# Powers of the query and key norms by logarithm and exponential on ScalarE, and the causal mask put on the logarithms

## The chip, the cores and the metric

The kernel runs on one core of a Trainium2 chip. A core has TensorE (PE in the profile; PEld is its weight load), VectorE (DVE), ScalarE (ACT), GpSimd (POOL) and SyncE (SP), each with a queue of its own that is worked off in order, and 16 DMA engines. The metric is device time in microseconds, lower is better; shown are the median of the runs of the kernel before and one execution taken by the hardware profiler.

## The reference, cut to what matters

One layer of a decoder trunk on 512 tokens of width 2048, all in float32. The part that the change touches is the attention branch with its two norms (8 heads of 128 features, blocks of 128 queries):

```python
def rmsnorm(x, g):
    y = x * lax.rsqrt(jnp.mean(x * x, axis=-1, keepdims=True) + EPS)
    return y * g

q = rmsnorm(q.reshape(B, S, 8, 128), q_norm_g)
k = rmsnorm(k.reshape(B, S, 8, 128), k_norm_g)

# stick-breaking attention, for one block of queries
z = einsum('bhqd,bhkd->bhqk', qi, kf) * 128 ** -0.5
strict = key_pos[None, :] < q_pos[:, None]
log_beta = log_sigmoid(z)
log_1m = where(strict, log_sigmoid(-z), 0)
tail = cumsum(log_1m, axis=3, reverse=True) - log_1m
w = where(strict, exp(log_beta + tail), 0)
out = einsum('bhqk,bhkd->bhqd', w, vf)
```

Around it stand a combined projection `w_in` (9216 columns: u, v_sgu, q, k, v_att and two gates), a gated spatial branch, the merge through `w_up_a`, `w_up_b` and `w_o`, a feed-forward block with 5632 hidden units, and a gated embedding.

## The kernel before, in words

Everything is kept transposed: features on the 128 partitions, the 512 tokens along the free dimension. A matrix product works on pairs of 128 output rows. Each float32 operand is split into a high part, copied to the fp32r type by ScalarE, and a low part, the rest, formed by VectorE; a product is the sum of three matmuls (high by high, high by low, low by high). Most products run on blocks with seven multiplications in place of eight (`PRODUCTS`, `HALVES`), whose sums of activations and weights VectorE forms; one sum of two weight blocks is formed by a DMA that adds into its destination (`landed`, L351, issued from GpSimd's queue once the first part of the weights has landed). `high`, `sums` and `rest` are the other steps of a piece of weights: L347 on ScalarE is the high part, L363 the sums, L344 the low part on VectorE. `mix_doubled` (L751 on ScalarE, L754 on VectorE) takes the seven products out of PSUM.

The projection goes first, for 56 pairs of output rows. The order is four rounds, each a pair of q (two heads), of k, of v and then three or four pairs of gates; after the rounds come the pairs of the gated spatial branch. The attention of a round runs beside the matmuls of the pairs that follow. Its steps are generators (`q_prep`, `k_prep`, `v_prep`, `attention`), and each `yield n` puts the next step n ticks later; there are eight ticks to a pair. Instructions that a tick issues are kept behind the matmuls issued before it. Within these limits the engines' orders come from a planner that estimates the duration of each instruction and gives a free engine the earliest step in the text whose inputs it reckons to be there. So the order on an engine can differ from the order in the text.

- `q_prep`: `flip` (L1032) transposes one head's queries so that tokens lie on partitions; `squares` (L1039) lets ScalarE square and sum each of the four blocks of tokens; `token_rms` forms the mean plus epsilon on VectorE (L1047) and raises it to the power -0.5 on GpSimd (L1049); VectorE multiplies the result by 128 ** -0.5 (L1064); one tick later `times` (L1054) scales the queries on ScalarE; two ticks later they are transposed back and ScalarE multiplies them by the gain (L1071).
- `k_prep` does the same for the keys up to the power, which is kept in `rk` and used as the scale of the logits (L1109, L1110). The first norm's epsilon is carried as `eps_cols`, four columns made once from the mean of squares of x (L1302), since the rows of x are not scaled ahead of the projection.
- `attention` goes through blocks of 128 keys, the last first, with the keys on partitions and the queries that can see the block along the free dimension. `stage_a` (L1107 to L1112) makes z and log(1 + exp(-|z|)). `stage_m` makes the logarithm of the weight `w` (L1116) and the sum term `s` (L1118) on VectorE; GpSimd sets s to zero where a key is not ahead of its query (L1120), copies one row out (L1127) and clears it (L1128). `stage_b` (L1131) and `stage_c` (L1135) split s into high and low parts; `stage_d` sums it over keys with a triangular matrix on TensorE (L1141, L1142), carries a row to the next block (L1144), subtracts the sums from w (L1146) and takes the exponential (L1147); GpSimd sets the weight to zero where the mask says so (L1148). `finish` multiplies the four blocks of weights with the values (L1157) and copies the result out (L1159).

PSUM has two banks for all small products of attention and six for the projection. The table set that ScalarE loads at the start is `natural_log_exp_and_others` (L852).

Of the kernel before, what the change touches and what calls it, by code (L numbers as in the profile page):

```python
# [12 lines left out]
F32 = mybir.dt.float32  # L13
F32R = mybir.dt.float32r
AF = mybir.ActivationFunctionType
ALU = mybir.AluOpType
# [3 lines left out]
P = 128  # L20
T = 512
NT = T // P
# [5 lines left out]
GROUPS = 8  # L28
PLE = 256
EPS = 1e-6  # L30

OUT = "SSSSPPPP"
PASSES = "SSSSSSSS", "SSSSSSSS", "SSSSPP"
# [34 lines left out]
def hybrid_layer(  # L68
# [18 lines left out]
    nc = tc.nc  # L87

    consts = ctx.enter_context(tc.tile_pool(name="consts", bufs=1))
# [810 lines left out]
    def load_x():  # L900
# [18 lines left out]
                            fill=0.0, base=0, channel_multiplier=1)  # L919
# [3 lines left out]
    expo = consts.tile([P, 8], F32, name="expo")  # L923
# [67 lines left out]
    norm1 = Norm()  # L991
# [32 lines left out]
        return att[tag].f(start, start + n)  # L1024

    eps_cols = consts.tile([P, NT], F32, name="eps_cols")

    def flip(o):

# [10 lines left out]
                                 accum_out=ms[:, t : t + 1])  # L1040
        return ms

    def token_rms(ps, r):

        norm1.row()
        ms = squares(ps)
        nc.vector.scalar_tensor_tensor(out=ms, in0=ms, scalar=1.0 / P, in1=eps_cols,  # L1047
                                       op0=ALU.mult, op1=ALU.add)
        nc.gpsimd.tensor_tensor(out=r, in0=ms, in1=expo[:, :NT], op=ALU.pow)  # L1049

    def times(dst, ps, r):
        for t in range(NT):
# [3 lines left out]
    def q_prep(o, i):  # L1056


        for h in range(2):
            yield 2  # L1060
            ps = flip(o[:, h * T : (h + 1) * T])
            q, r = take(T), rms_tile()[:, :NT]
            token_rms(ps, r)
            nc.vector.tensor_scalar(out=r, in0=r, scalar1=float(P) ** -0.5, scalar2=None,  # L1064
                                    op0=ALU.mult)
            yield 1
            times(q.f(), ps, r)
            yield 2
            if not h:
                y_b[i] = take(1024)  # L1070
            nc.scalar.activation(y_b[i].f(h * T, (h + 1) * T), flip(q.f()), AF.Copy,  # L1071
                                 scale=gcol[:, g_q : g_q + 1])
            give(q)
# [12 lines left out]
    def attention(rnd, kT, rk, v):  # L1086
        state = {}
        yield 1
        qT = y_b[rnd].f()
        zh, zl = (att[t].own() for t in ("zh", "zl"))  # L1090

        def sums(j):
            return a_tile("zs", (NT - j) * P, j % 2 * T)

        def weights(h, j):
            return a_tile(f"w{j}", (NT - j) * P, (j == NT - 1) * h * P)

        def first(j):

            return (sums(j) if j == NT - 1 else a_tile("first", (NT - j) * P, (j == 1) * 2 * P))[0:1]  # L1100

        def stage_a(h, j):
            n = (NT - j) * P
            r = rk[:, 4 * h + j : 4 * h + j + 1]
            z = small_bank()[:, :n]
            c = h * T + j * P
            nc.tensor.matmul(z, kT[:, c : c + P], qT[:, c : (h + 1) * T], start=True, stop=True)  # L1107
            l, s = a_tile("l")[:, :n], sums(j)
            nc.scalar.activation(l, z, AF.Abs, scale=r)  # L1109
            nc.scalar.activation(s, z, AF.Copy, scale=r)  # L1110
            nc.scalar.activation(l, l, AF.Exp, scale=-1.0)
            nc.scalar.activation(l, l, AF.Ln, bias=1.0)  # L1112

        def stage_m(h, j):
            l, s, w = a_tile("l")[:, : (NT - j) * P], sums(j), weights(h, j)
            nc.vector.scalar_tensor_tensor(out=w, in0=s, scalar=0.0, in1=l,  # L1116
                                           op0=ALU.min, op1=ALU.subtract)
            nc.vector.scalar_tensor_tensor(out=s, in0=s, scalar=0.0, in1=l,  # L1118
                                           op0=ALU.max, op1=ALU.add)
            nc.gpsimd.affine_select(out=s[:, :P], in_=s[:, :P], pattern=[[1, P]],  # L1120
                                    compare_op=ALU.is_gt, fill=0.0, base=0,
                                    channel_multiplier=-1)


            if j < NT - 1:
                if j:
                    nc.gpsimd.tensor_copy(first(j), s[0:1])  # L1127
                nc.gpsimd.memset(s[0:1, :P], 0.0)  # L1128

        def stage_b(j):  # L1130
            nc.scalar.activation(zh[:, : (NT - j) * P], sums(j), AF.Copy)  # L1131

        def stage_c(j):
            n = (NT - j) * P
            in_turn(nc.vector.tensor_tensor(out=zl[:, :n], in0=sums(j), in1=att["zh"].f(0, n),  # L1135
                                            op=ALU.subtract))

        def stage_d(h, j):
            n, w = (NT - j) * P, weights(h, j)
            tp, t = small_bank()[:, :n], tris[j < NT - 1]  # L1140
            nc.tensor.matmul(tp, t, zh[:, :n], start=True, stop=False)  # L1141
            nc.tensor.matmul(tp, t, zl[:, :n], start=False, stop=True)  # L1142
            if j:
                nc.vector.tensor_tensor(out=sums(j - 1)[0:1, P:], in0=tp[0:1], in1=first(j),  # L1144
                                        op=ALU.add)
            nc.vector.tensor_tensor(out=w, in0=w, in1=tp, op=ALU.subtract)  # L1146
            nc.scalar.activation(w, w, AF.Exp)  # L1147
            nc.gpsimd.affine_select(out=w[:, :P], in_=w[:, :P], pattern=[[1, P]],  # L1148
                                    compare_op=ALU.is_gt, fill=0.0, base=0,
                                    channel_multiplier=-1)  # L1150
            state[h, "w", j] = w

        def finish(h):
            y = small_bank()
            for j in range(NT):
                c = h * T + j * P
                nc.tensor.matmul(y[:, j * P :], v[:, c : c + P], state.pop((h, "w", j)),  # L1157
                                 start=j == 0, stop=j == NT - 1)
            nc.scalar.activation(qT[:, h * T : (h + 1) * T], y, AF.Copy)  # L1159
            if h == 1:  # L1160
                nc.sync.dma_start(out=y_spill[rnd], in_=qT)
                give(y_b[rnd])
                y_done["b", rnd] = True

        blocks = [(h, j) for h in range(2) for j in range(NT - 1, -1, -1)]
        stage_a(*blocks[0])
        yield 1
        stage_m(*blocks[0])
        yield 1
        stage_a(*blocks[1])  # L1170
        for i, (h, j) in enumerate(blocks):
            ahead = blocks[i + 1 : i + 3]
            stage_b(j)
            yield 1
            if i == NT:
                finish(0)
            stage_c(j)
            if ahead:
                stage_m(*ahead[0])
            yield 1  # L1180
            stage_d(h, j)
            if ahead[1:]:
                stage_a(*ahead[1])
            yield 1
        yield 1
        finish(1)
        if rnd == 3:
            for tag in ("first", "k", "v", "zs", "zh", "zl"):
                give(att.pop(tag))

    def sgu_v(rnd, o):

        for h in range(2):
# [10 lines left out]
            ssq = squares(ps)  # L1204
            nc.vector.tensor_scalar(out=ssq, in0=ssq, scalar1=1.0 / P, scalar2=EPS,
                                    op0=ALU.mult, op1=ALU.add)
# [92 lines left out]
    for n, ((w, i), pr) in enumerate(zip(order, made())):  # L1299
        if n == 0:  # L1300
            row1 = norm1.row()
            nc.vector.tensor_scalar(out=eps_cols, in0=norm1.mean, scalar1=EPS, scalar2=None,  # L1302
                                    op0=ALU.mult)
        if n == 0:
            a_tiles()
        o = pr.out(block(w, i) if n < 3 else None)
        if w == "q":
            beside(q_prep(o, i))
        elif w == "k":
            kT, rk = o, rms_tile()  # L1310
            beside(k_prep(kT, rk))
            beside(attention(i, kT, rk, a_tile("v", 1024)), 6)
        elif w == "v":
            beside(v_prep(o, a_tile("v", 1024)))
        elif w == "s":
            scaled(o, row1)
            nc.scalar.activation(o, o, AF.Gelu_apprx_tanh)
            beside(sgu_v(i, o))
        elif w == "u":
            scaled(o, row1)  # L1320
            nc.scalar.activation(o, o, AF.Gelu_apprx_tanh)
            nc.vector.tensor_tensor(out=y_a[i].f(), in0=o, in1=y_a[i].f(), op=ALU.mult)
            y_done["a", i] = True
        else:
            d = tc.dram_tile([P, 1024], F32, name=nm("gsp"))
            nc.sync.dma_start(out=d, in_=o)
            gate_spill[w, i] = d
# [5 lines left out]
    ms = [form(k, lambda j=j: merged[j], lambda j=j: j in merged, raw=0, **how)  # L1333
          for j, k in enumerate(OUT) for how in [{} if k == "S" else {"how": "high"}]]
# [232 lines left out]
```

## Time and profile before

| | us |
|---|---|
| median of 3 runs | 2690.93 |
| lowest, highest | 2689.34, 2696.23 |
| profiled execution | 2691.74 |
| its span, first to last instruction | 2690.0 |

How to read the profile: "busy" is the sum of an engine's instruction times; a matmul's end is modelled. In a table of stretches, the columns are the length, the busy time of PE, PEld, DVE, ACT and POOL with counts, the clock that TensorE was granted as a share of full speed, the share of the DMA engines' time and GB/s. In a row of waits stand the engine that waited, tile and line, what released it, then total us, times and the longest. A row of the timeline has start, duration, engine, line, instruction, shapes, count, and in brackets the idle time ahead of it with its releaser. A row of a group has count, busy us and mean ns of one, then the idle time of the engine ahead of it. A row of one line's durations has the lowest, median and highest in ns. An engine's idle time costs nothing where it isn't the one that sets the end.

### The profile page before, as it was taken

To read this page: it belongs to the slowest core of one execution; us is meant where nothing else is said; L and a number is where in the kernel's file an instruction comes from. 1 tells how busy PE (TensorE), PEld (TensorE's weight loads), DVE (VectorE), ACT (ScalarE), POOL (GpSimd) and SP (SyncE) were. 2 spreads that over 40 slices of the span, in tenths; PEclk is the share of its full clock that TensorE was granted. 3 is DMA by queue.
4 is the path that set the end of the run, shared out by engine and by line. 5 is a ranking of instruction groups with operands and counts; after the bars stand their busy time and mean duration, and the time that the engine had idled before them with its cause. 6 is when DMAs were issued, how large, how long until landed. Compare 5 with 4: busy or idle time off the path is not lost.

```text
span 2690.0 us, 42553 instructions
## 1 busy us (share of the span) xinstructions
PE 2653.3 (99%) x15496; PEld 2325.7 (86%) x15496; DVE 2207.7 (82%) x3715; ACT 1388.7 (52%) x2161; POOL 458.2 (17%) x549
## 2 busy tenths in 40 slices
PE   8999999999999999999999999999999999999999
PEld 7889898889898889988888888888888888888898
DVE  8687878787887666688898888888899889889876
ACT  7656565655554334375444444444445444444543
POOL 0223323232220000001111111111110111100010
PEclk9999999999999999999999999999999999999999
DMA  7677777777776457667888888888888979978884
GB/s 226 154 185 175 182 173 184 172 183 198 174 187 196 140 164 211 178 210 198 230 212 213 204 202 200 201 206 199 207 197 244 259 213 279 259 254 259 257 248 126
DMA packets 288241, 548.62 MB, mean 204 GB/s; under 512 B 25888, under 2 KB 138272, under 8 KB 288032
## 3 DMA queue, kind: packets, MB, share of 16 engines
q1 hardware_dynamic: 229232, 441.03, 50.3%
q0 software_dynamic: 58800, 104.88, 25.2%
q8 instruction: 121, 1.98, 0.3%
q14 instruction: 88, 0.72, 0.1%
HBM read 498.63 MB, written 47.19 MB: 203 GB/s over the span
## 4 chain that ended last, share of the span: by engine, by line
PE 85%; DVE 7%; DMA 3%; ACT 2%; issue 2%; POOL 1%; SPq 0%; DVEq 0%; ACTq 0%; POOLq 0%
PE ps L695 47%; PE ps L285 10%; PE ps L286 10%; PE ps L284 10%; PE small L695 6%; DVE wlo L344 2%; DVE out L754 1%; DMA wholes<-x 1%; DVE parts L275 1%; PE small L1157 1%; DMA wholes<-hid 1%; DVE wholes L363 1%; ACT whi L347 1%; DVE wholes L513 1%; PE small L1032 1%
## 5 line engine op out<-in xcount | busy, mean ns | idle before, releaser
L695 PE MATMUL ps<-parts,whi 128*128 128x512 f32 x3960 | 1324.8, 397 | 0.3 <-DVE p L754 0.3
L347 ACT ACTIVATE whi<-wholes 128x512 fp32r<-128x512 f32 (+3 forms) x933 | 866.0, 942 | 787.0 <-DVE wholes L363 274.0
L344 DVE TENSOR_TENSOR wlo<-wholes,whi 128x512 fp32r<-128x512 f32 (+3 forms) x933 | 974.1, 1078 | 85.6 <-ACT whi L347 85.4
L695 PEld LDWEIGHTS ps<-parts,wlo 128*128 128x128 f32 x3960 | 743.7, 188 | 168.1 <-issue 1.0
L695 PE MATMUL ps<-parts,wlo 128*128 128x256 f32 x3960 | 784.3, 279 | 0.1
L285 PE MATMUL ps<-parts,whi 128*128 128x256 f32 (+1 forms) x2070 | 679.5, 329 | 4.8 <-DVE parts L275 4.7
L284 PE MATMUL ps<-parts,whi 128*128 128x256 f32 (+1 forms) x2048 | 668.1, 328 | 12.4 <-ACT parts L274 10.6
L286 PE MATMUL ps<-parts,wlo 128*128 128x256 f32 (+1 forms) x2070 | 677.6, 329 | 1.7 <-DVE wlo L344 1.7
L695 PEld LDWEIGHTS ps<-parts,whi 128*128 128x128 f32 x3960 | 637.8, 189 | 5.9 <-issue 1.0
L285 PEld LDWEIGHTS ps<-parts,whi 128*128 128x128 f32 x2070 | 393.6, 190 | 46.5 <-DVE parts L275 7.3
L284 PEld LDWEIGHTS ps<-parts,whi 128*128 128x128 f32 x2048 | 388.5, 190 | 48.9 <-ACT parts L274 12.7
L286 PEld LDWEIGHTS ps<-parts,wlo 128*128 128x128 f32 x2070 | 393.5, 190 | 36.2 <-DVE wlo L344 3.2
L363 DVE TENSOR_TENSOR wholes<-wholes 128x256 f32<-128x256 f32 (+1 forms) x806 | 338.9, 420 | 19.1 <-issue 1.7
L754 DVE TENSOR_TENSOR out<-out,ps 128x256 f32<-128x256 f32 x460 | 190.8, 417 | 150.9 <-ACT out L751 150.2
L351 POOL DMA_DIRECT2D wholes<-w_ffn_in x172 | 150.1, 872 | 689.1 <-DVE wholes L363 251.7
L351 POOL DMA_DIRECT2D wholes<-w_in x132 | 118.3, 898 | 484.4 <-DMA wholes<-w_in 133.7
L695 PE MATMUL small<-parts,whi 128*128 128x512 f32 x440 | 174.5, 397 | 0.0
L275 DVE TENSOR_TENSOR parts<-wholes,parts 128x1024 fp32r<-128x1024 f32 (+4 forms) x134 | 131.0, 989 | 17.6 <-ACT parts L274 17.6
L274 ACT ACTIVATE parts<-wholes 128x1024 fp32r<-128x1024 f32 (+4 forms) x134 | 112.9, 865 | 46.9 <-DVE wholes L513 26.1
L351 POOL DMA_DIRECT2D wholes<-w_ffn_out x64 | 55.8, 872 | 402.5 <-DMA wholes<-w_ffn_out 101.6
L751 ACT ACTIVATE out<-ps 128x256 f32<-128x256 f32 x243 | 91.4, 385 | 47.5 <-PE ps L695 44.0
L1403 ACT ACTIVATE out<-out 128x512 f32<-128x512 f32 x44 | 27.9, 633 | 156.3 <-DVE out L1402 156.3
(120 smaller groups left out, 1721.6 us busy)
## 6 DMA issues: line engine op xcount, KB each, us to landing
wholes<-w_ffn_in SPq DMA_DIRECT2D x172, 384.0 KB, 5.6
wholes<-w_in SPq DMA_DIRECT2D x132, 384.0 KB, 5.0
wholes<-w_ffn_in SPq DMA_DIRECT2D x172, 256.0 KB, 4.8
wholes<-w_ffn_in POOLq DMA_DIRECT2D x172, 256.0 KB, 5.5
wholes<-w_in SPq DMA_DIRECT2D x132, 256.0 KB, 4.2
wholes<-w_in POOLq DMA_DIRECT2D x132, 256.0 KB, 4.9
wholes<-w_ffn_out SPq DMA_DIRECT2D x64, 384.0 KB, 5.4
wholes<-hid SPq DMA_DIRECT2D x42, 512.0 KB, 5.8
```

Source lines behind the costliest of these rows:

```text
L274: return (nc.scalar.activation(hi, src, AF.Copy), nc.vector.tensor_tensor(out=lo, in0=src, in1=hi.bitcast(F32), op=ALU.subtract))
L275: nc.vector.tensor_tensor(out=lo, in0=src, in1=hi.bitcast(F32), op=ALU.subtract))
L284: nc.tensor.matmul(ps, sh, mh, start=start, stop=False)
L285: nc.tensor.matmul(ps, sh, ml, start=False, stop=False)
L286: return nc.tensor.matmul(ps, sl, mh, start=False, stop=stop)
L344: in_turn(nc.vector.tensor_tensor(out=self.lo[:, blocks], in0=r, in1=h.bitcast(F32), op=ALU.subtract))
L347: in_turn(nc.scalar.activation(h, r, AF.Copy))
L351: nc.gpsimd.dma_start(out=raw[:, 3:5], in_=self.src[:, 1:3], accum_op=ALU.add)
L363: in_turn(nc.vector.tensor_tensor(out=o, in0=x, in1=y, op=ALU.add))
L695: m = nc.tensor.matmul(out, l, r, start=first and k == 0, stop=last and k == 1)
L751: in_turn(nc.scalar.activation(out, x, AF.Copy, scale=scale))
L754: in_turn(nc.vector.tensor_tensor(out=out, in0=x, in1=y, op=op))
```

## The change

Three edits. First, `token_rms` takes the power -0.5 as exp(-0.5 ln(.)) with two ScalarE activations on the four columns, in place of one GpSimd instruction. Second, the factor 128 ** -0.5 of the queries is folded in: `q_prep` passes the sum of squares unscaled with an epsilon 128 times as large (a second tile, `eps_q`, made beside `eps_cols`), and VectorE's multiplication of the result goes. Third, the mask on the weights behind the exponential (L1148) goes, and a mask with the value -10000 is put on their logarithms at the end of `stage_m`; the exponential then gives zero there.

```diff
+MASKED = -1e4
...
+    eps_q = consts.tile([P, NT], F32, name="eps_q")
...
-    def token_rms(ps, r):
+    def token_rms(ps, r, scale=1.0 / P, eps=eps_cols):
 
         norm1.row()
         ms = squares(ps)
-        nc.vector.scalar_tensor_tensor(out=ms, in0=ms, scalar=1.0 / P, in1=eps_cols,
+        nc.vector.scalar_tensor_tensor(out=ms, in0=ms, scalar=scale, in1=eps,
                                        op0=ALU.mult, op1=ALU.add)
-        nc.gpsimd.tensor_tensor(out=r, in0=ms, in1=expo[:, :NT], op=ALU.pow)
+        nc.scalar.activation(ms, ms, AF.Ln)
+        nc.scalar.activation(r, ms, AF.Exp, scale=-0.5)
...
             q, r = take(T), rms_tile()[:, :NT]
-            token_rms(ps, r)
-            nc.vector.tensor_scalar(out=r, in0=r, scalar1=float(P) ** -0.5, scalar2=None,
-                                    op0=ALU.mult)
+            token_rms(ps, r, 1.0, eps_q)
...
                 nc.gpsimd.memset(s[0:1, :P], 0.0)
+            nc.gpsimd.affine_select(out=w[:, :P], in_=w[:, :P], pattern=[[1, P]],
+                                    compare_op=ALU.is_gt, fill=MASKED, base=0,
+                                    channel_multiplier=-1)
...
             nc.scalar.activation(w, w, AF.Exp)
-            nc.gpsimd.affine_select(out=w[:, :P], in_=w[:, :P], pattern=[[1, P]],
-                                    compare_op=ALU.is_gt, fill=0.0, base=0,
-                                    channel_multiplier=-1)
...
-            nc.vector.tensor_scalar(out=eps_cols, in0=norm1.mean, scalar1=EPS, scalar2=None,
-                                    op0=ALU.mult)
+            for eps, c in ((eps_cols, EPS), (eps_q, EPS * P)):
+                nc.vector.tensor_scalar(out=eps, in0=norm1.mean, scalar1=c, scalar2=None,
+                                        op0=ALU.mult)
```

## The prediction

> **What bounds the kernel now.** I read the busy shares first, then the stretch in which the changed lines run (the first power of a query norm starts at 100 us, the last mask ends at 599 us), then TensorE's own waits in that stretch, then each of them in order of time.
>
> ```profile
> span 2690.0 us, 42553 instructions
> ...
> PE 2653.3 (99%) x15496; PEld 2325.7 (86%) x15496; DVE 2207.7 (82%) x3715; ACT 1388.7 (52%) x2161; POOL 458.2 (17%) x549
> ```
> ```profile
> core 0: us, PE busy (x) PEld busy (x) DVE busy (x) ACT busy (x) POOL busy (x), PEclk, DMA share, GB/s
> 90.00:605.00 515.00, 505.93 (x3171) 445.65 (x3171) 409.53 (x757) 317.72 (x672) 161.30 (x212) 1.00 0.73 178
> ```
> TensorE (PE) sets the end: it is idle for 36.7 us of the span, and for 515.00 - 505.93 = 9.07 us of this stretch, which holds four rounds of two heads each. A change that touches only this stretch can win that, and what a lowered clock costs, and no more. VectorE (DVE) is 80% busy there, ScalarE (ACT) 62%, GpSimd (POOL) 31%. The waits of TensorE that lead to the changed lines, with their total, count and longest:
>
> ```profile
> PE small L1142 <- DVE parts L1135: 3.4, 4, 0.9
> PE small L1032 <- ACT wholes L1054: 2.2, 1, 2.2
> PE small L1157 <- POOL wholes L1148: 2.2, 4, 0.6
> ```
> The last two end at operations that the change removes or moves. The first ends at VectorE's low part of the sums (L1135), downstream of GpSimd's mask of the sums.
>
> **The removed power.** This is the one pause at L1032, in the first round, in order of time:
>
> ```profile
> 97.03 0.16 DVE L1047 SCALAR_TENSOR_TENSOR ms<-ms,eps_cols 128x4 f32<-128x4 f32 x1 [1.61 <-ACT sq L1039]
> ...
> 98.52 0.67 ACT L347 ACTIVATE whi<-wholes 128x512 fp32r<-128x512 f32 x1
> ...
> 99.85 0.88 POOL L351 DMA_DIRECT2D wholes<-w_in  x1 [2.84 <-DMA wholes<-w_in]
> ...
> 100.43 1.38 POOL L1049 TENSOR_TENSOR rr<-ms,expo 128x4 f32<-128x4 f32 x1
> ...
> 100.85 0.40 PE L695 MATMUL ps<-parts,whi 128*128 128x512 f32 x1
> 101.84 0.17 DVE L1064 TENSOR_SCALAR rr<-rr 128x4 f32<-128x4 f32 x1 [4.64 <-POOL rr L1049]
> ...
> 102.04 0.37 ACT L1054 ACTIVATE wholes<-small,rr 128x128 f32<-128x128 f32 x1 [2.85 <-DVE rr L1064]
> 102.31 1.13 ACT L1054 ACTIVATE wholes<-small,cols 128x128 f32<-128x128 f32 x4
> 103.31 0.91 ACT L1054 ACTIVATE wholes<-small,rr 128x128 f32<-128x128 f32 x3
> ...
> 103.50 0.66 PE L1032 MATMUL small<-ident,wholes 128*128 128x128 f32 x4 [2.25 <-ACT wholes L1054]
> ```
> ```profile
> 100.00:104.00 4.00, 1.75 (x12) 1.26 (x10) 2.16 (x4) 1.96 (x8) 2.24 (x3) 1.00 0.58 86
> 104.00:108.00 4.00, 3.88 (x19) 3.54 (x18) 0.93 (x3) 2.63 (x10) 1.63 (x2) 0.57 0.54 164
> ```
> The mean of squares is ready at 97.19, but the power stands in GpSimd's queue behind a weight transfer that waits until 99.85 for its first part to land. The power ends at 101.8, VectorE's multiplication by a constant follows, then the scaling on ScalarE, and TensorE, done at 101.25, starts the transposes at 103.50. The granted clock of the next 4 us (the third number from the right) is 0.57, so (1 - 0.57) x 4.00 = 1.72 us more are lost.
>
> Sixteen powers and eight multiplications go; sixteen logarithms and sixteen exponentials on four columns come. No row shows that shape on ScalarE; these are the nearest, beside the power's own and a table load:
>
> ```profile
> L1049 POOL TENSOR_TENSOR rr<-ms,expo 128x4 f32<-128x4 f32 x16 | 24.2, 1511 | 3.3 <-DVE ms L1047 3.3
> ...
> L1039 ACT ACTIVATION_READ_ACCUMULATOR sq<-small 128x1 f32 x96 | 19.0, 198 | 0.0
> ...
> L1111 ACT ACTIVATE wholes<-wholes 128x512 f32<-128x512 f32 x8 | 5.0, 627 | 0.0
> ...
> L1111 ACT ACTIVATE wholes<-wholes 128x128 f32<-128x128 f32 x8 | 2.5, 316 | 0.0
> ...
> L852 ACT ACT_TABLE_LOAD x1 | 1.3, 1283 | 0.8 <-PEq L1557 0.8
> ```
> The two exponentials give (627 - 316) / 384 = 0.81 ns an element, so an estimate for 4 elements is 316 - 124 x 0.81 = 216 ns; the bounds are 198 and 316 ns. I take 0.22 us: 32 x 0.22 = 7.0 us on ScalarE (6.3 to 10.1), which has 515 - 317.7 = 197 us free there. GpSimd loses 24.2 us; VectorE loses 8 x 0.17 = 1.4 us and gains one more 4-column row of epsilons (0.2 us, before 90 us). None of these totals is on the path; the order is.
>
> In the first round, if ScalarE first runs the weight copies that it ran then (until 99.19), logarithm, exponential and four scalings (0.44 + 0.37 + 0.91) end at 100.91, before TensorE arrives at 101.25. If it also runs the value tiles' scaling ahead of them (1.13 us, as at 102.31), they end at 102.04 and 0.8 us of the pause is left. I take it as gone: -2.25, and the clock's loss with it: -1.72. The low end of this gain is 1.4 us, with the clock lowered all the same; a loss needs a new hold on ScalarE, which is a rival below.
>
> [...]
>
> **The moved mask.** In every round the last product of weights and values waits for GpSimd's mask behind the last exponential. The second round's end is typical:
>
> ```profile
> 325.58 0.63 ACT L1147 ACTIVATE wholes<-wholes 128x512 f32<-128x512 f32 x1 [4.91 <-DVE wholes L1146]
> ...
> 326.29 1.15 POOL L1148 TENSOR_SCALAR_AFFINE_SELECT wholes<-wholes 128x128 f32<-128x128 f32 x1 [0.47 <-ACT wholes L1147]
> ...
> 327.49 2.42 PE L1157 MATMUL small<-wholes 128*128 128x512 f32 x8 [0.57 <-POOL wholes L1148]
> ```
> Without the mask there, the weights are ready at 326.21 and TensorE arrives at 326.92: the wait goes, with 0.7 us in hand. Four times, that is -2.2 us by the wait row above. ScalarE's exponential is next in that chain and not late.
>
> The mask itself does not vanish. It moves to where the logarithms are made, beside another mask of the same size on the same engine, where the chain to the round's other pause (L1142) runs:
>
> ```profile
> 304.51 0.55 DVE L1116 SCALAR_TENSOR_TENSOR wholes<-wholes 128x384 f32<-128x384 f32 x1
> ...
> 305.32 0.55 DVE L1118 SCALAR_TENSOR_TENSOR wholes<-wholes 128x384 f32<-128x384 f32 x1
> ...
> 305.95 2.41 POOL L1120 TENSOR_SCALAR_AFFINE_SELECT wholes<-wholes 128x128 f32<-128x128 f32 x1 [3.52 <-DVE wholes L1118]
> ...
> 306.12 2.09 DVE L344 TENSOR_TENSOR wlo<-wholes,whi 128x1280 fp32r<-128x1280 f32 x2
> ...
> 308.42 0.50 POOL L1127 COPY wholes<-wholes 1x384 f32<-1x384 f32 x1
> ...
> 308.95 0.41 DVE L1144 TENSOR_TENSOR wholes<-small,wholes 1x256 f32<-1x256 f32 x1 [0.75 <-POOL wholes L1127]
> ```
> ```profile
> DVE wholes L1144 <- POOL wholes L1127: 4.6, 7, 1.0
> ```
> ```profile
> L1120 POOL TENSOR_SCALAR_AFFINE_SELECT wholes<-wholes x32: 284/407/2414, 121.0 to 585.9; 128x128 f32<-128x128 f32 x32
> ```
> In the text the new mask stands behind the old mask, the copy and the memset. But its input (L1116) is ready before theirs (L1118), and the planner does put a later step first where its input is ready: the value tiles' scaling at 102.31 ran between two pieces of the query's. So I assume that the new mask runs first. It then costs the sums between nothing (it runs under L1118) and 2.41 us (it sits under VectorE's 2.09 us pair, as the old one did here, and the old one is caught again by the next). I take the median of the last row, 0.41 us, since a mask held up under that pair lets both out together. The delay reaches TensorE where VectorE waits for L1127 on the way to a round's last blocks; I count that once a round: 4 x 0.41 = +1.6 us. Behind the new mask on GpSimd stand the copy, the memset and the weight transfers; these lose less than they gain by the 1.15 us mask and the 1.5 us powers that leave their queue. SyncE's queue is not touched.
>
> [...]
>
> **Sum.** -2.25 - 1.72 - 2.2 + 1.6 = -4.6 us. From the profiled execution, 2691.74 us (the span of 2690.0 and 1.7 around it), that is 2687.1; the median shown, 2690.93, is 0.8 us lower, so I forecast 2686.3 us. About what a measurement of this kernel can tell from no change is 0.3%, or 8.1 us: the forecast lies inside it.
>
> **Rivals.**
> - *All the idle time goes*: the chain also runs ahead of L1142. Price: -9.07 - 1.72 = -10.8, so 2680.1 us. For it: VectorE no longer waits 4.64 us at L1064. Against it: the L1142 waits come out of VectorE's backlog, which is not shortened.
> - *The gain is eaten*: part of the first round's pause stays and the masks take back the rest: 2689 to 2692 us.
> [...]
> - *ScalarE is held up.* The logarithm waits in ScalarE's queue for VectorE's mean of squares, and weight copies, PSUM copies and attention's exponentials stand behind it:
>
> ```profile
> 116.05 0.20 ACT L1039 ACTIVATION_READ_ACCUMULATOR sq<-small 128x1 f32 x1
> ...
> 117.60 0.15 DVE L1047 SCALAR_TENSOR_TENSOR ms<-ms,eps_cols 128x4 f32<-128x4 f32 x1
> ```
> Here VectorE comes 1.35 us late; sixteen such holds that all reach TensorE are +21.6 us, less 4.6, so 2707.9 us. The kernel is slower by 0.3% from 0.8 us a hold at TensorE. Against it: ScalarE is 38% idle and the weights are split ahead of their use.
> - *Tables*: if logarithm and exponential needed different tables, 32 x 1.283 = 41.1 us would come, 2727 us. Against it: attention alternates both (L1111, L1112), and the profile has no load at those lines.
>
> **How the numbers follow.** Forecast (2684 to 2689) 0.47; gain eaten 0.15; all idle time 0.12; masks under VectorE 0.12, a third of it above +8.1 us; ScalarE held up 0.12; tables, or an order that opens a pause with a lowered clock in each round (4 x 3.97 = 16 us), 0.02. Faster by over 0.3%: 0.12. Slower: 0.04 + 0.12 + 0.02 = 0.18. Within: 0.70. The range runs from all idle time gone (2680) to 2698, short of the slower cases.
>
> **What would show it.** Right: no TensorE wait at L1032 near 101 us and no clock below 1.00 from 104 to 108; no L1157 wait on GpSimd; on GpSimd the mask of w ahead of the mask of s; an L1142 wait of 1.2 us a round. Wrong: a new TensorE wait behind ScalarE (L347 or L751) in each round, table loads beside the new lines, or a difference beyond 605 us, where no changed instruction runs.

## The result and the profile after

The kernel after takes 2686.52 us (median of 20 runs, 2681.96 to 2691.56), the kernel before 2692.16 us in its 20 runs (2686.38 to 2696.23). The ratio is 0.9982, 95% interval 0.9975 to 0.9989: 3.0 to 6.7 us less, where 4.6 were forecast. The difference is smaller than the 0.3% of the prediction, but a ratio of 1 lies outside the interval. The profiled execution of after took 2687.82 us.

Lines of after are one to four further down than those of before: the flips are L1034, the mean of squares L1049, logarithm and exponential of the power L1051 and L1052, the scaling L1057, the mask of the sums L1121, the new mask L1130, the parts of the sums L1135 (ScalarE) and L1139 (VectorE), the sums L1146, the exponential of the weights L1151, the product with the values L1158, weights copies L348, low parts L345, landed sums L352, products out of PSUM L755. In the kernels of the experiments the same operations stand within five lines of these.

First the page of after, then its table of stretches, both with the columns that the prediction has:

```profile
span 2686.1 us, 42603 instructions
...
PE 2652.4 (99%) x15496; PEld 2325.8 (87%) x15496; DVE 2209.0 (82%) x3708; ACT 1391.2 (52%) x2193; POOL 436.2 (16%) x533
```
```profile
90.00:605.00 515.00, 507.95 (x3212) 449.31 (x3210) 413.08 (x752) 323.28 (x705) 140.79 (x198) 1.00 0.73 181
100.00:104.00 4.00, 4.00 (x32) 3.72 (x31) 0.74 (x2) 3.98 (x13) 0.07 (x1) 1.00 0.89 220
104.00:108.00 4.00, 4.00 (x27) 3.50 (x26) 1.74 (x6) 4.00 (x16) 0.80 (x1) 1.00 0.49 82
```
From 100 to 108 us TensorE is now busy throughout at a clock of 1.00, where before it had 1.75 and 3.88 us, the second at a clock of 0.57. GpSimd lost 22.0 us of busy time (458.2 to 436.2), ScalarE gained 2.5 (1388.7 to 1391.2), and TensorE's total is unchanged within 0.9 us. TensorE's waits in the stretch, and the first round in order of time:

```profile
PE small L1158 <- ACT wholes L1151: 2.5, 3, 0.9
PE small L1146 <- DVE parts L1139: 2.4, 4, 1.3
PE small L1108 <- ACT wholes L1057: 0.9, 3, 0.3
PE small L1158 <- issue: 0.8, 1, 0.8
...
```
```profile
97.52 0.23 ACT L1051 ACTIVATE ms<-ms 128x4 f32<-128x4 f32 x1
...
97.86 0.24 ACT L1052 ACTIVATE rr<-ms 128x4 f32<-128x4 f32 x1
...
98.48 0.41 ACT L1057 ACTIVATE wholes<-small,rr 128x128 f32<-128x128 f32 x1
...
98.76 0.88 POOL L352 DMA_DIRECT2D wholes<-w_in  x1 [2.60 <-DMA wholes<-w_in]
...
99.77 0.38 ACT L1057 ACTIVATE wholes<-small,cols 128x128 f32<-128x128 f32 x1
...
100.31 0.60 PE L1034 MATMUL small<-ident,wholes 128*128 128x128 f32 x4
```
The weight transfer still waits for its first part (2.60 us, until 98.76), but the power no longer stands behind it. The query's scaling starts at 98.48 and no longer at 102.04, the value tiles' scaling behind it (`cols`) ends at 100.15 and no longer at 103.44, and the transposes that follow at 100.31 (103.50 before) have no idle time ahead of them. Both waits that ended at removed or moved operations (L1032 behind the scaling, L1157 behind GpSimd's mask) are gone; in their place stands one that was not in the list before, the product L1158 behind ScalarE's exponential (two rows, four times, 3.3 us in all). The prediction's signs of being wrong named a new wait of TensorE behind ScalarE in each round, at the weight copies or the copies out of PSUM; one came in each round, but at the exponential.

**A finer measure.** The time of a whole run of after varies by 9.6 us from one execution to another, so the experiments are read by one stretch as well: from the first transposition of a query to the last start of the product of weights and values, in the table of stretches. By the counts of matmuls (3121 to 3123) TensorE has the same work in it in each kernel. The start of the stretch lies between 93.6 and 95.3 us in the twelve executions, and what differs ahead of it isn't counted:

```profile
94.60:601.70 507.10, 498.03 (x3122) 438.56 (x3121) 402.81 (x747) 314.36 (x666) 158.43 (x208) 1.00 0.72 177
```
```profile
93.80:595.00 501.20, 494.15 (x3121) 436.81 (x3120) 403.39 (x739) 317.62 (x698) 136.53 (x192) 1.00 0.73 179
```
The first row is before, the second after: 507.1 and 501.2 us with 3122 and 3121 matmuls. Length less busy time is TensorE's idle time: 9.07 and 7.05 us. Since a matmul's end is modelled, the split of a gain between busy and idle time is rough; the length is not. Each row of the table is one profiled execution; the ratio beside it is that of whole times. The table holds this for every kernel, and where the four rounds end (last start of that product in each round, counted from the start of the stretch).

| kernel | stretch, us | busy | idle | ends of rounds | ratio to before, 95% |
|---|---|---|---|---|---|
| before | 507.1 | 498.0 | 9.1 | 99.1, 235.0, 371.1, 507.1 | |
| before again (c1_before, run once) | 507.3 | 498.0 | 9.3 | 99.3, 235.4, 371.4, 507.3 | |
| after | 501.2 | 494.2 | 7.0 | 94.1, 229.4, 364.9, 501.2 | 0.9982, 0.9975 to 0.9989 |
| after again (c2_after, run once) | 500.6 | 494.2 | 6.4 | 93.9, 229.3, 365.2, 500.6 | |
| e1_powers_only | 502.1 | 495.4 | 6.7 | 94.4, 230.5, 366.3, 502.1 | 0.9980, 0.9971 to 0.9988 |
| e2_mask_only | 504.2 | 495.0 | 9.2 | 98.2, 233.6, 368.9, 504.2 | 0.9996, 0.9987 to 1.0005 |
| e3_mask_last | 500.4 | 494.3 | 6.1 | 93.5, 229.2, 364.7, 500.4 | 0.9975, 0.9966 to 0.9984 |
| e4_no_mask | 501.0 | 494.6 | 6.4 | 92.8, 227.8, 365.4, 501.0 | 0.9979, 0.9969 to 0.9989 |
| e5_first_only | 503.5 | 496.2 | 7.3 | 95.3, 231.2, 367.2, 503.5 | 0.9988, 0.9979 to 0.9997 |
| e7_double | 506.0 | 496.2 | 9.8 | 98.1, 233.4, 369.5, 506.0 | 0.9989, 0.9979 to 0.9999 |
| e8_pause8 | 505.0 | 495.0 | 10.0 | 96.7, 232.7, 368.5, 505.0 | 0.9982, 0.9973 to 0.9991 |
| e9_pause4 (run once) | 502.2 | 495.4 | 6.8 | 95.9, 231.0, 366.7, 502.2 | |

### The profile page after: what moved, and what is told of

Read it like the earlier page. It is cut to its first block, busy times and chain, and to the rows that moved or that the text cites. A ratio compares the mean times of both kernels' runs of the same rounds, so it can differ in the third digit from the quotient of the medians.

```text
span 2686.1 us, 42603 instructions
## 1 busy us (share of the span) xinstructions
PE 2652.4 (99%) x15496; PEld 2325.8 (87%) x15496; DVE 2209.0 (82%) x3708; ACT 1391.2 (52%) x2193; POOL 436.2 (16%) x533
## 4 chain that ended last, share of the span: by engine, by line
PE 84%; DVE 7%; DMA 3%; ACT 3%; issue 2%; POOL 1%; SPq 0%; POOLq 0%; DVEq 0%; ACTq 0%
PE ps L696 46%; PE ps L287 10%; PE ps L286 10%; PE ps L285 10%; PE small L696 6%; DVE wlo L345 3%; DVE out L755 1%; DVE parts L276 1%; ACT whi L348 1%; DMA wholes<-hid 1%; PE small L1158 1%; PE small L1034 1%; DMA wholes<-w_in 1%; DVE wholes L364 1%; DVE wholes L514 1%
## 5 line engine op out<-in xcount | busy, mean ns | idle before, releaser
L348 ACT ACTIVATE whi<-wholes 128x512 fp32r<-128x512 f32 (+3 forms) x933 | 866.5, 941 | 782.8 <-DVE wholes L364 268.2
L345 DVE TENSOR_TENSOR wlo<-wholes,whi 128x512 fp32r<-128x512 f32 (+3 forms) x933 | 976.1, 1080 | 86.4 <-ACT whi L348 85.8
L755 DVE TENSOR_TENSOR out<-out,ps 128x256 f32<-128x256 f32 x460 | 190.5, 417 | 154.1 <-ACT out L752 154.0
L352 POOL DMA_DIRECT2D wholes<-w_ffn_in x172 | 150.1, 873 | 690.3 <-DVE wholes L364 219.9
L352 POOL DMA_DIRECT2D wholes<-w_in x132 | 116.3, 882 | 528.5 <-DMA wholes<-w_in 118.9
L352 POOL DMA_DIRECT2D wholes<-w_ffn_out x64 | 55.8, 872 | 402.4 <-DMA wholes<-w_ffn_out 100.1
```

What stands on the lines that cost most here:

```text
L345: in_turn(nc.vector.tensor_tensor(out=self.lo[:, blocks], in0=r, in1=h.bitcast(F32), op=ALU.subtract))
L348: in_turn(nc.scalar.activation(h, r, AF.Copy))
L352: nc.gpsimd.dma_start(out=raw[:, 3:5], in_=self.src[:, 1:3], accum_op=ALU.add)
L755: in_turn(nc.vector.tensor_tensor(out=out, in0=x, in1=y, op=op))
```

## The experiments

### The same two kernels once more

No edit: c1_before is the kernel before, c2_after the kernel after.

> The kernel before once more, for its trace. If the stretch from the first transposition to the last product of weights and values is a property of the kernel, it is 507.1 us within 0.5, with the pause near 101 us. The lowered clock behind the pause is open: the kernel with the moved mask alone had a pause of 2.9 us at this place with the clock at 1.00. If the clock follows from the pause alone it is 0.57 again; if it hangs on chance as well, the stretch may come out up to 1.7 us shorter.

> The kernel after once more, for its trace: 501.2 us within 0.5 if the stretch is a property of the kernel, with the fourth round again 0.8 to 1 us longer than the second and third (136.3 against 135.3 and 135.5); if that round is chance, it comes down to 135.4 and the stretch to 500.4.

Measured: the stretch took 507.3 and 500.6 us, against 507.1 and 501.2 the first time, so two executions of a kernel lie 0.2 and 0.6 us apart, a difference of about 1 us can be told, and the change brings 5.9 to 6.7 us there. The fourth round of after, 136.3 us the first time, took 135.4 in the repeat: its extra length was scatter. Whole times scatter more: 2693.03 us for before, 2680.57 for after, 2687.82 in the first execution of after. Most of that lies behind the attention. The last of the eight transfers to the tile "sum" (L1438) starts at 2205.9 us in after and at 2204.7 in its repeat. Up to there the two executions differ by 1.2 us; from there to the end of the span they took 480.2 (2686.1 - 2205.9) and 474.2 us (2678.9 - 2204.7), and before 476.9 and 476.5 (from 2213.1 and 2214.8, L1436). From the end of the stretch to that transfer all four take nearly the same: 1611.4 and 1612.2 us in before, 1610.9 and 1610.2 in after. So it is the same kernel that takes 6 us more or less at the end, and no step of the change is judged by that part; a gain beyond 605 us, the last sign of being wrong, isn't shown.

The pause of the first round recurs in the second execution of before, with the clock behind it (waits, then the table of stretches):

```profile
PE small L1032 <- ACT wholes L1054: 2.4, 1, 2.4
```
```profile
104.00:108.00 4.00, 3.44 (x15) 3.01 (x16) 1.87 (x5) 3.34 (x13) 1.41 (x2) 0.64 0.63 177
108.00:112.00 4.00, 4.00 (x28) 3.73 (x27) 0.58 (x2) 3.31 (x9) 1.96 (x2) 0.94 0.52 70
```
(1 - 0.64) x 4.00 + (1 - 0.94) x 4.00 = 1.68 us, against 1.72 in the first execution.

### One part at a time

e1_powers_only: after, with the mask on the weights back behind the exponential.

```diff
-            nc.gpsimd.affine_select(out=w[:, :P], in_=w[:, :P], pattern=[[1, P]],
-                                    compare_op=ALU.is_gt, fill=MASKED, base=0,
-                                    channel_multiplier=-1)
...
             nc.scalar.activation(w, w, AF.Exp)
+            nc.gpsimd.affine_select(out=w[:, :P], in_=w[:, :P], pattern=[[1, P]],
+                                    compare_op=ALU.is_gt, fill=0.0, base=0,
+                                    channel_multiplier=-1)
```

> The powers by logarithm and exponential and the folded factor alone; the mask stays behind the exponential. Measure: from the first transposition of a query (L1032 before) to the last product of weights and values (L1157), 507.1 us in the kernel before and 501.2 us after the whole change. My theory: the pause of 2.25 us near 101 us and the lowered clock behind it go, about -4.0 us, 503.1 us; the four waits of L1157 on GpSimd (0.54 to 0.57 us) stay. Rival, the gain comes from the mask: -1 us or less, 506 us or more.

e2_mask_only: before, with the mask moved the same way and the powers left on GpSimd (the edit above, backwards, in before).

> The moved mask alone; the power stays on GpSimd. My theory: -2.2 us by the four waits at the rounds' ends, +1.6 us by the mask ahead of the mask of the sums, so -0.6 us, 506.5 us for the same stretch; the pause of 2.25 us and the clock of 0.57 stay. Rival, the mask brings all that the powers leave of the measured -5.9 us: -1.9 us, 505.2 us.

Measured: the stretch fell by 5.0 us with the powers alone (to 502.1; 503.1 was expected) and by 2.9 with the mask alone (to 504.2; neither the 506.5 of the theory nor the 505.2 of the rival). In whole times the second can't be told from no change (0.9987 to 1.0005). The waits of the first, then the waits and two stretches of the second:

```profile
PE small L1143 <- DVE parts L1136: 3.5, 4, 0.9
PE small L1158 <- POOL wholes L1149: 2.1, 4, 0.5
```
```profile
PE small L1033 <- ACT wholes L1055: 2.9, 1, 2.9
PE small L1158 <- ACT wholes L1151: 2.5, 3, 0.9
...
PE small L1146 <- DVE parts L1139: 0.8, 2, 0.5
```
```profile
100.00:104.00 4.00, 1.38 (x8) 0.93 (x7) 1.35 (x2) 1.14 (x5) 1.95 (x2) 1.00 0.72 111
104.00:108.00 4.00, 3.57 (x26) 3.21 (x27) 1.75 (x5) 3.97 (x13) 1.54 (x2) 1.00 0.58 175
```
With the powers alone the first pause is gone and the four waits for the mask are still there (2.1 us); with the mask alone it is the other way round. So each wait belongs to the part to which the prediction put it. The powers alone bring 5.0 us where the whole change brings 5.9 to 6.7, nearly all of it (4.7) in the first round.

The two parts alone add up to 7.9 us, and together they bring 5.9 to 6.7. One difference is to be seen: in e2 the first pause was longer than in before (2.9 us), and yet the clock stayed at 1.00. Had it fallen as in before, e2 would have lost 1.72 us more and won 1.2; 5.0 + 1.2 = 6.2 fits the sum. That is worked out, not tried.

### The first power alone

e5_first_only: before, with logarithm and exponential for the first query norm only; the other fifteen powers stay on GpSimd.

```diff
-    def token_rms(ps, r):
+    def token_rms(ps, r, first=False):
...
-        nc.gpsimd.tensor_tensor(out=r, in0=ms, in1=expo[:, :NT], op=ALU.pow)
+        if first:
+            nc.scalar.activation(ms, ms, AF.Ln)
+            nc.scalar.activation(r, ms, AF.Exp, scale=-0.5)
+        else:
+            nc.gpsimd.tensor_tensor(out=r, in0=ms, in1=expo[:, :NT], op=ALU.pow)
...
-            token_rms(ps, r)
+            token_rms(ps, r, first=i == 0 and h == 0)
```

> The kernel before, with logarithm and exponential for one norm only: the first query head of the first round. All other powers, VectorE's factor and the late mask stay. My theory (the whole gain of the powers is the one pause near 101 us): the stretch from the first transposition to the last product of weights and values is 507.1 us before and 502.1 us with all sixteen powers exchanged; this one comes within 0.5 of 502.1, and nearly all of it in the first round (99.1 us before, 94.4). Rival, GpSimd and VectorE are freed in each round: half of the gain or less, 504.6 us or more.

Measured: 503.5 us, 3.6 less than before, all of it in the first round (3.8). The theory had 502.1 within 0.5, the rival 504.6 or more; it lies between. The pause and the lowered clock are gone (table of stretches of e5):

```profile
100.00:104.00 4.00, 4.00 (x29) 3.49 (x28) 2.29 (x6) 3.78 (x14) 1.94 (x2) 1.00 0.82 162
104.00:108.00 4.00, 4.00 (x29) 3.62 (x28) 0.58 (x2) 4.00 (x15) 1.96 (x2) 1.00 0.80 181
```
One norm of sixteen brings nearly what the prediction worked out for it (2.25 + 1.72 = 3.97). Against the mean of the two executions of before (9.21 idle, 497.99 busy), idle time fell by 1.9 us and busy time by 1.8, near the pause and the clock. The order on ScalarE changed as well: in e5 the value tiles' scaling (from 100.30) runs ahead of the query's (from 101.32). So what is shown is that the exchange of this one power removes the pause, by an earlier power and by the order that the planner makes with it together. The other fifteen powers and VectorE's eight multiplications, counted at nothing, bring the rest of e1's gain: 503.5 - 502.1 = 1.4 us, 0.9 of it still in the first round.

### The price of the new mask

e3_mask_last: after, with the new mask held behind the mask of the sums, the copy and the clearing on GpSimd; an order only, no wait is added.

```diff
-            nc.gpsimd.affine_select(out=w[:, :P], in_=w[:, :P], pattern=[[1, P]],
+            m = nc.gpsimd.affine_select(out=w[:, :P], in_=w[:, :P], pattern=[[1, P]],
...
+            tc.add_manual_dep(
+                m.ins, last.ins.name,
+                mybir.DependencyInfo(mybir.DependencyClass.NoSync,
+                                     mybir.DependencyReason.DATA),
+                reason="behind the mask of the sums")
```

> The whole change, with GpSimd's new mask held behind the mask of the sums, the copy and the memset by an order on GpSimd's queue. If the new mask's place in front costs what I put on it (4 x 0.41 us), the stretch falls from 501.2 to 499.6 us. Rival: GpSimd is shut out by VectorE's long instructions whichever mask comes first, and nothing moves: 501.2 us within 0.5.

e4_no_mask: after, without any mask on the weights; the kernel leaves out their causal mask.

```diff
-            nc.gpsimd.affine_select(out=w[:, :P], in_=w[:, :P], pattern=[[1, P]],
-                                    compare_op=ALU.is_gt, fill=MASKED, base=0,
-                                    channel_multiplier=-1)
```

> The whole change, but no mask at all on the weights: the kernel leaves out the causal mask of w (the mask of the sums stays). It prices the new mask on GpSimd. My theory (it costs 1.6 us): 499.6 us. Rival: it also makes the four new waits of L1158 in the middle of the rounds (0.8 to 0.9 us each), so these go with it: 497.8 us. Second rival: it costs nothing, 501.2 us.

Measured: 500.4 us with the mask last and 501.0 without it, against 501.2 and 500.6 with the mask in front. The 499.6 that both kernels would have shown if the new mask cost 1.6 us didn't come: it costs nothing in the sum that can be told from scatter, and neither does its place. The new waits in the middle of the rounds look like this in after, in the second round:

```profile
281.90 2.81 POOL L1130 TENSOR_SCALAR_AFFINE_SELECT wholes<-wholes 128x128 f32<-128x128 f32 x1
...
282.47 2.08 DVE L345 TENSOR_TENSOR wlo<-wholes,whi 128x1280 fp32r<-128x1280 f32 x2
...
284.67 0.29 POOL L1121 TENSOR_SCALAR_AFFINE_SELECT wholes<-wholes 128x128 f32<-128x128 f32 x1
...
284.99 0.31 ACT L1135 ACTIVATE parts<-wholes 128x128 fp32r<-128x128 f32 x1 [0.99 <-POOL wholes L1121]
...
286.67 0.61 ACT L1151 ACTIVATE wholes<-wholes 128x512 f32<-128x512 f32 x1
...
287.43 2.39 PE L1158 MATMUL small<-wholes 128*128 128x512 f32 x8 [0.84 <-ACT wholes L1151]
```
The new mask runs first and takes 2.81 us beside VectorE's pair of low parts; the mask of the sums, which the next block needs, follows at 284.67; ScalarE stands 0.99 us for it, and the exponential of the first head's last weights, queued behind it, comes late for TensorE by 0.84 us. But the delay on GpSimd isn't new. In before the old mask lies at the same place of the round, as long and also ahead of the mask of the sums:

```profile
287.65 2.75 POOL L1148 TENSOR_SCALAR_AFFINE_SELECT wholes<-wholes 128x128 f32<-128x128 f32 x1
...
290.36 0.29 POOL L1120 TENSOR_SCALAR_AFFINE_SELECT wholes<-wholes 128x128 f32<-128x128 f32 x1
...
291.39 0.62 ACT L1147 ACTIVATE wholes<-wholes 128x512 f32<-128x512 f32 x1
291.91 0.29 ACT L1131 ACTIVATE parts<-wholes 128x128 fp32r<-128x128 f32 x1
```
There ScalarE runs the exponential first (L1147) and its part of the sums behind it (L1131), so TensorE doesn't wait. In after the order is the other way round: L1135 at 284.99, L1151 at 286.67. In every round, before and its repeat, e1, e4 and e5 have the exponential first and no wait of TensorE in mid-round; after and its repeat, e2, e3, e7 and e8 have the sums first and the wait. In all of them a mask runs beside that pair of VectorE and takes 2.0 to 4.0 us (2.61 to 3.14 us in the four rounds of before, 2.81 to 2.96 us in those of after). So the wait comes with the order on ScalarE, which changed with the moved mask (e2 has the new order, e1 and e4 the old one); how late the mask of the sums ends then seems to set its length. With the mask last these waits shrink, and the ones at the round's end grow (waits of e3):

```profile
PE small L1151 <- DVE parts L1144: 3.3, 4, 1.0
PE small L1163 <- ACT wholes L1156: 1.5, 3, 0.5
...
PE small L1163 <- issue: 0.4, 1, 0.4
```
1.5 + 0.4 in place of 2.5 + 0.8 us in mid-round, 3.3 in place of 2.4 at the sums. Without the mask (e4) the waits in mid-round are gone, and 2.4 us at L755, VectorE's copies out of PSUM, have come. What one chain gives back, another seems to take. The best median is e3's (2684.61 us), but its interval overlaps that of after, so it isn't told from it.

### ScalarE's load

e7_double: after, with logarithm and exponential taken twice for each norm (the result is that of the second pair).

```diff
-        nc.scalar.activation(ms, ms, AF.Ln)
-        nc.scalar.activation(r, ms, AF.Exp, scale=-0.5)
+        for _ in range(2):
+            g = small(NT)
+            nc.scalar.activation(g, ms, AF.Ln)
+            nc.scalar.activation(r, g, AF.Exp, scale=-0.5)
```

> The whole change, with logarithm and exponential taken twice: 32 more instructions of 0.22 us on ScalarE, 7 us in all. My theory (ScalarE has room, only the order counts): the stretch of 501.2 us grows by 0.5 us or less. Rival, ScalarE's queue is on the path: by up to 7 us.

Measured: 506.0 us, 4.8 to 5.4 more than after and its repeat, 4.0 to 4.2 of it in the first round; at most 0.5 was expected. Whole times do not tell e7 from after (0.9979 to 0.9999 against 0.9975 to 0.9989), so this rests on one execution. The pair that is added costs ScalarE 32 x 0.206 = 6.6 us by its durations; TensorE loses 4.8 to 5.4, most of it in one pause and the clock behind it (waits of e7, and the stretch behind it):

```profile
PE ps L696 <- DVE out L755: 2.8, 1, 2.8
```
```profile
136.00:140.00 4.00, 3.84 (x13) 3.32 (x14) 3.54 (x8) 3.13 (x7) 0.00 (x0) 0.57 0.17 31
```
The chain of waits that leads to it (start, length, what) starts at a doubled pair and goes through two weight transfers, GpSimd's queue and VectorE:

```profile
115.38 0.20 ACT ms L1053
...
116.02 0.19 ACT rr L1054
116.20 0.78 ACT whi L348
116.98 4.50 DMA wholes<-w_in
...
125.02 1.42 DVE wlo L345
...
126.45 6.12 DMA wholes<-w_in
...
133.24 0.89 POOL wholes L352
134.13 0.33 POOL wholes L1123
...
135.77 0.34 DVE out L755
```
By this chain the pair delays ScalarE's copy of weights and with it the next weights; these land later, and at 132.6 GpSimd's queue stands for a transfer (L352) with the mask of the sums behind it (in e7 it is L1123). VectorE's copy of a product out of PSUM comes behind that, and TensorE waits 2.8 us and then runs at 0.57. In after the mask of that block had run at 127.11, ahead of its transfer. So 0.4 us more on ScalarE per norm are enough, in the first round, to open a pause at another place. As the order on GpSimd changed with it, this run doesn't separate the delay from the order.

### The pause itself

e8_pause8 and e9_pause4: after, with eight or four scalings on ScalarE behind the first norm, whose result is overwritten.

```diff
             token_rms(ps, r, 1.0, eps_q)
+            for t in range(8 if i == 0 and h == 0 else 0):
+                nc.scalar.activation(q.f(0, P), ident, AF.Copy, scale=r[:, 0:1])
```

> The whole change, with eight more ScalarE scalings of 128 columns (0.25 to 0.37 us each, 2 to 3 us) between the first query head's power and its scaling, so that a pause of TensorE like the one of the kernel before comes back near 101 us. My theory, that the pause costs its own length and a lowered clock: a pause of 2 us or more, the granted clock of the next 4 us near 0.57, and the first round longer than 94.1 us by the pause and 1.7 us. Rival, the clock of the kernel before was lowered by something else: clock 1.00, the first round longer by the pause alone.

> The same with four scalings (1 to 1.5 us): a pause of about 1 us. Pauses of 0.9 us at the rounds' ends left the clock at 1.00, so I expect 1.00 here and a first round longer than 94.1 us by the pause alone. Rival, the clock falls after any pause at this place.

Measured: 505.0 us with eight and 502.2 with four, but not by the pause that they were to bring back, so neither theory nor rival was put to the test. With eight, the transposes start at 102.13, right behind the value tiles' scaling, which the added work delays, and TensorE has no gap ahead of them (timeline and stretches of e8):

```profile
101.65 0.37 ACT L1057 ACTIVATE wholes<-small,cols 128x128 f32<-128x128 f32 x1
...
102.13 0.60 PE L1034 MATMUL small<-ident,wholes 128*128 128x128 f32 x4
```
```profile
100.00:104.00 4.00, 4.00 (x30) 3.68 (x29) 1.70 (x5) 3.94 (x18) 0.81 (x1) 1.00 0.80 163
136.00:140.00 4.00, 2.43 (x13) 1.87 (x14) 3.97 (x8) 2.54 (x5) 0.00 (x0) 1.00 0.48 110
```
TensorE got other work to do in the meantime; a gap of 1.5 us came at 136 to 140. The order is made with durations that the planner knows, and with work that it sees on ScalarE it put other matmuls ahead of the transposes. In before, by this reading, the pause came from what it could not see: a queue of GpSimd that waits for a transfer to land. That the planner's knowledge is the difference is argued from its description and from these two rows; the transfer's wait alone wasn't taken away. What the pause costs by itself at a given length isn't settled by these two runs.

## Why the prediction was right

- **The forecast** was 4.6 us less, the runs show 3.0 to 6.7, the stretch 5.9 to 6.7 (501.2 and 500.6 against 507.1 and 507.3). The sign, the place and the main cause hold. That the median, 2686.52, lies 0.2 us from the forecast 2686.3 is in part luck: the forecast started from 2690.93, the kernel before has 2692.16 in twenty runs, and the two medians are 5.6 us apart.
- **The removed power** (-2.25 and -1.72): right in size. No wait at the transposes near 101 us, clock 1.00, and e5 wins 3.6 us with this one norm. One link was read wrongly. "VectorE's multiplication by a constant follows, then the scaling on ScalarE, and TensorE, done at 101.25, starts the transposes at 103.50" takes the query's scaling for the release; but three of its four blocks ran from 103.31 on, behind the value tiles' scaling, which ended at 103.44 (102.31 + 1.13), 0.06 us ahead of the transposes. The code gives attention two banks of PSUM; by these times the transposes waited for the bank that the value tiles' scaling frees (inferred, no run takes it apart), and the late power held them up only by standing at the head of ScalarE's queue.
- **ScalarE's part**: 0.22 us each was the estimate, 0.206 and 0.205 us are the means of after, with no table load among them. Busy time of ScalarE in the stretch grew by 3.3 us (314.36 to 317.62), not by 7.0, as neighbours on ScalarE overlap: the exponential at 97.86 ends at 98.10, and the next instruction starts at 97.96. That this is hidden was right, but with less to spare than the 197 us of free time suggest: e7. ScalarE's rival was put down as sixteen small holds that all reach TensorE; what the doubling showed is one pause in the first round, by a chain through the weights, together with another order on GpSimd.
- **The other fifteen powers** and the eight multiplications, counted at nothing, bring 1.4 us, by one execution each of e5 and e1. This is a term that was mis-sized. The prediction said of the totals "None of these totals is on the path; the order is" and then priced the order at one place. Which waits the 1.4 us come from isn't shown.
- **The four waits for the late mask** (-2.2): right, none is left in after. They also seem to cost a little in the matmuls behind them, which the sum did not hold. The product on 512 columns, in before, after and e4, by groups (count, busy us, mean ns, idle us ahead):

```profile
L1157 PE MATMUL small<-wholes 128*128 128x512 f32 x16 | 9.0, 644 | 2.2 <-POOL wholes L1148 2.2
```
```profile
L1158 PE MATMUL small<-wholes 128*128 128x512 f32 x16 | 8.5, 611 | 3.3 <-ACT wholes L1151 2.5 <-issue 0.8
```
```profile
L1155 PE MATMUL small<-wholes 128*128 128x512 f32 x16 | 8.2, 591 | 0.0
```
  With no wait ahead of it the group takes 591 ns, in after 611, in before 644: 16 x 33 ns = 0.5 us less from before to after. In e1 and e5, with the late mask, it takes 645 and 644 ns, in e2 and e3 611, though e3's waits are shorter (1.9 us in all); why the two kinds of wait differ stays open.
- **The new mask's order and price** (+1.6 at L1142): the order was right, its size and the place of the price wrong. GpSimd does run the mask of w ahead of the mask of s. The new mask has a median of 0.64 us, not 0.41, and 2.81 to 2.96 us at the place in mid-round where it lies beside VectorE's pair; that is the case of the chance "masks under VectorE 0.12", in one place of each round. No run shows the loss of over 8.1 us in which a third of that chance was put: the stretch took 501.2 us with the new mask and 501.0 without it (e4). But the wait at the sums was forecast at 1.2 us a round and fell, from 3.4 us in all to 2.4 (1.6 in the repeat). The price came in mid-round, at the first head's product behind the exponential: 2.5 us and 0.8 under "issue", 3.3 in all. The step that failed is "the delay reaches TensorE where VectorE waits for L1127": the delay at this place was there in before too (2.75 us), and what changed is ScalarE's order, its part of the sums now standing ahead of the exponential that TensorE needed. In this step the prediction weighed GpSimd's order alone. By idle time in the list of waits the moved mask is then -2.2 - 1.0 + 3.3 = +0.1 us where -2.2 + 1.6 = -0.6 was said. By the length of the stretch it brings 0.9 to 1.5 us on top of the powers (e1's 502.1 against 501.2 and 500.6), with idle time nearly the same (6.7 against 7.0 and 6.4): that gain shows in the busy time, 0.5 us of it at the product above, the rest unexplained.
- **The sum by kind**: forecast were -2.85 us of idle time and -1.72 of busy time. Measured, as means of two executions each: idle 9.21 to 6.73, busy 497.99 to 494.17, so -2.5 and -3.8. The idle part is right by two terms that were off in opposite directions: a price in another place, and waits at the sums that fell. In the busy part 1.7 us are the clock, 0.5 the product above, and about 0.7 the other fifteen powers with the multiplications (e5 496.18, e1 495.44 us); the 0.9 us that are left are spread over 3121 matmuls whose ends are modelled, and stay open.

In the second round of after a mask took 2.81 us beside VectorE's pair (L1130) and one of the same size 0.29 us behind it (L1121). Whether anyone waits for the long one is decided elsewhere: with the same delay on GpSimd (2.75 us in that round), before has no wait of TensorE in mid-round and after has four of under 1 us.

## What to carry to other kernels

Price a small operation by the queue in which it stands, not by its duration alone: taking a 1.4 us power from behind a transfer that had not landed brought 3.6 us, and as two activations of 0.2 us on ScalarE it left no wait of TensorE at that place. When a step is moved, compare the order on every engine before and after, not only on the one that it leaves or enters: a delay of 2.8 us on GpSimd was there in both kernels, and it reached TensorE only where ScalarE's part of the sums had come to stand ahead of an exponential that does not use it. And where whole times scatter by more than the change is worth, compare one stretch with equal matmul counts between two executions of the same kernel first; here they agreed within 0.6 us.

## What the runs showed of the hardware

In these executions the clock's fall isn't set by the length of the pause alone. Behind pauses of 2.25 us (before), 2.4 us (its repeat) and 2.8 us (e7) the next 4 us had 0.57, 0.64 and 0.57; behind 2.9 us in e2 they had 1.00. In before the four slices of 1 us from 104 to 108 had 0.63, 0.50, 0.50 and 0.67, and the slices on both sides 1.00. What was lost, by the clock of slices of 4 us, is 1.72, 1.68 and 1.72 us, with no more behind the longer pause than behind the shorter. A price for the clock (1.7 us) is therefore one that a pause of this length can have, not one that it must. What decides between the two isn't shown.
